# Pinning the output projection's first two passes between the steps of attention, and moving x2's first transposes

## The chip, the cores and the metric

The kernel runs on one core of one Trainium2 chip. The metric is the device time in microseconds of one execution. The time before is the median of three runs, 719.41 us (718.87 to 719.6).

## The reference

One layer of a hybrid decoder on x of 512 tokens by 1024 features, float32:

```python
h = rms_norm(x, norm_mix); proj = h @ w_in
y_a = gdn_mixer(...)      # 6 heads, gated DeltaNet: chunk solves and a scan
y_b = nsa_mixer(...)      # 6 heads, 3 per key/value head
y_c = pool_mixer(...)     # causal pooling, 4 windows
y = concatenate([y_a, y_b, y_c])          # 384 + 384 + 256 = 1024
x = x + y @ w_out
h = rms_norm(x, norm_ffn)
x = x + square(relu(h @ w_ffn1)) @ w_ffn2
```

In `nsa_mixer` each head adds three attentions: over compressed blocks, over selected blocks (with 512 tokens all blocks are chosen, so it is causal attention) and over a window of 512 (causal attention again, with other keys and values), each times a gate. What matters here is that each of the six heads needs two softmaxes over 512 x 512 causal scores and their products with the values, and that `y @ w_out` sums over eight blocks of 128 features: blocks 0 to 2 from DeltaNet, 3 to 5 from attention (two heads each), 6 and 7 from pooling.

## The kernel before, in words

**Stages.** Input projection, DeltaNet solves and scan, compression and pooling run until about 241 us. Then `gdn_out` (line 922) turns the four row blocks of the DeltaNet output, and line 1272 runs two tracks beside each other: `attentions()` and `out_gdn()`, the first part of the output projection. Lines 1311 to 1320 finish the projection, norm the sum x2 (`x2_norm`, line 1277) and transpose it (`x2_T`, line 1296); line 1334 on is the FFN, which takes the rest of the span.

**Who sets the order.** The Python code traces instructions; `side_by_side` (line 945) interleaves the tracks by the costs that they yield and their weights, a yield of -1 meaning "blocked until another track has traced what I need" (`until`, line 996). Then a scheduler of the framework gives each engine its order: it runs the traced program on a clock of its own and takes, for each engine, the earliest traced instruction that is ready. On the chip each engine then works through its own list in that order. `kp` (line 150) pins an instruction behind the one traced just before it on its engine, so that the scheduler can't move it ahead. Instructions that aren't pinned can still be taken earlier.

**Attention.** A step is one head and one of two branches (h, br), twelve steps in all. `probs` (line 1102) makes, for each of four row blocks, scores in one of two PSUM banks (0 and 1): two matmuls and a mask matmul (lines 1110 to 1112), a maximum on VectorE (1114), an exponential on ScalarE (1116); then the sums are turned into scales (1119, 1120), and two blocks are scaled on VectorE (1125) and two on ScalarE (1123). `values` (line 1127) works through three groups of blocks (`BLKS`): transposes on TensorE into bank 2 or 6 (1139), a copy to high parts on ScalarE and the rest on VectorE (`split_rows`, 147 and 148; the third group a plain copy, 1142), then the products (1155) into the head's bank. `in_turn` mixes one step's `values` with the next step's `probs`. A head's bank alternates between 7 and 3 (`pa`, line 1064); it is begun by the compressed branch's product (1179) and read by `finish` (1184).

**The DeltaNet output.** `gdn_out` transposes each row block into bank 3 (`go`, line 70; line 936) and splits it in three pieces, each a copy on ScalarE and a subtraction on VectorE (line 938 through 147 and 148).

**The output projection.** `PASS` (line 1220) has three passes over feature blocks: (6, 7), (0, 1, 2), (3, 4, 5). `out_mm` (line 1227) issues three matmuls for each feature block (1233): high by high, high by low, low by high. `out_tile` does one row block and one half of the columns and adds it to x2 on VectorE (1238); a pass has eight such tiles. Passes one and two run in `out_gdn`, unpinned: 48 and 72 matmuls. The third is begun inside the very last step (5, 1): `out_begin` pins the first two feature blocks of four tiles there, one tile behind each group's transposes; the rest is pinned from line 1312 on, with `x2_T(0)` behind the fifth tile and `x2_T(1)` behind the seventh. Weights come by `load_w` (line 1204): a DMA on SP's queue into one of two raw buffers, then a ScalarE copy and a VectorE subtraction. Blocks 4 to 7 share four tiles, blocks 0 to 3 six. Behind the projection's weights `out_gdn` loads the first two of the FFN (line 1270). PSUM banks of the pieces are `po` (line 1225): 4 and 5 for pass one, 4, 5 and 6 for pass two, 4, 5, 0, 1 for pass three.

Of the kernel before, what the change touches and what calls it, by code (L numbers as in the profile page):

```python
# [20 lines left out]
P = 128  # L21
T = 512
D = 1024
NT = T // P
# [13 lines left out]
def trunk_kernel(ctx, tc, x, norm_mix, w_in, conv_w, a_log, dt_bias, gdn_norm, nsa_q_norm, nsa_k_norm,  # L38
# [18 lines left out]
    def banks(*ids):  # L57

        c = [0]

        def get():
            b_ = ids[c[0] % len(ids)]
            c[0] += 1
            return bank.tile([P, 512], F32, tag=f"b{b_}", name=nm("ps"))

        return get
# [282 lines left out]
    ps = pn()  # L349
# [595 lines left out]
    def side_by_side(*tracks):  # L945


        tracks = [[0.0, n, g] for n, g in tracks]
        while tracks:
            blocked = set()  # L950
            while True:
                if len(blocked) == len(tracks):
                    blocked.clear()
                t = min((t for t in tracks if id(t) not in blocked), key=lambda t: t[0] / t[1])
                c = next(t[2], None)
                if c is None:
                    tracks.remove(t)
                    break
                if c >= 0:
                    t[0] += c  # L960
                    break
                blocked.add(id(t))
# [33 lines left out]
    def until(*names):  # L996
        while not have.issuperset(names):
            yield -1
# [128 lines left out]
    def values(acc, h, br, Ps):  # L1127

        end = (h, br) == (H - 1, 1)
        keep = kp if end else lambda m: m
        if end:
            yield from until("w_out")
        for b, blks in enumerate(BLKS):
            n = len(blks) * P
            tp = pt_()
            for c, (k, i) in enumerate(blks):
                keep(PE.transpose(tp[:, ts(c, P)], Ps[i][:, ts(k, P)], ident))  # L1139
            if b == 2:  # L1140
                pt = [nw.tile([P, n], F32, tag=f"pt{b}", name=nm("pt"))]
                S.copy(pt[0], tp[:, :n])
            else:
                pt = [nw.tile([P, n], F32R, tag=f"pt{c}{b}", name=nm("pt")) for c in "hl"]
                split_rows(pt[0], pt[1], tp[:, :n])
            yield 0.4
            if end:
                out_begin()
            c = 0
            while c < len(blks):  # L1150
                k, i = blks[c]
                m = sum(1 for x_ in blks if x_[0] == k)
                for p_ in pt:
                    v_ = Vt[k][:, 2 * br + h // 3]
                    keep(PE.matmul(acc[0:64 if b == 2 else P, i * P:(i + m) * P],  # L1155
                                   v_ if b == 2 else v_.rearrange("p c d -> p (c d)"),
                                   p_[:, c * P:(c + m) * P], start=False, stop=(br == 1 and b == 2),
                                   skip_group_check=True))
                c += m
            yield 0.4  # L1160
        if end:
            out_begin()

    def attentions():
        G.memset(f32v(VCz), 0.0)
        for h in range(H):
            r = slice(32 * (h % 3), 32 * (h % 3) + 32)
            S.copy(VCz[r, h], f32v(VC[r, h // 3]).rearrange("p c d -> p (c d)"))
        last = iter(())
        for h in range(H):  # L1170
            if h % 3 == 0:
                pcT[h // 3] = cmp_probs(h // 3)
            acc = pa()
            for br in range(2):
                Ps = []
                yield from in_turn((probs(h, br, Ps), last))
                if br == 0:
                    for n_, p_ in enumerate(pcT[h // 3]):
                        PE.matmul(acc, VCz[:, h], p_, start=n_ == 0, stop=False, skip_group_check=True)
                last = values(acc, h, br, Ps)  # L1180
            last = finish(last, h, acc)
        yield from last
# [32 lines left out]
    def load_wo(*cs):  # L1215
        for c in cs:
            wo[c] = load_w(wop[c < 4], w_out[0, ts(c, P), :].unsqueeze(1), "wo", "AV")

    w1s = []
    PASS = [(6,7),(0,1,2),(3,4,5)]  # L1220

    def load_w1(q):
        return load_w(wq, w_ffn1[0, :, 256 * q:256 * q + 256].rearrange("(k p) n -> p k n", p=P), "w1", "AV")

    po = banks(4, 5), banks(4, 5, 6), banks(4, 5, 0, 1)

    def out_mm(ps, cl, n0, n1, i, hf, keep=lambda m: m):

# [7 lines left out]
    def out_add(ps, i, hf):  # L1236
        cs = slice(512 * hf, 512 * hf + 512)
        V.tensor_tensor(x2[i][:, cs], ps, x2[i][:, cs], ALU.add)

    def out_tile(cl, i, hf):  # L1240
        ps = po[cl[-1] < 6]()
        out_mm(ps, cl, 0, len(cl), i, hf)
        out_add(ps, i, hf)

# [2 lines left out]
    def out_begin():  # L1247

        g_ = len(begun)
        begun.append(po[2]())  # L1250
        out_mm(begun[g_], PASS[-1], 0, 2, g_ // 2, g_ % 2, kp)

    def out_part(cl, hf):

        for i in range(NT):
            out_tile(cl, i, hf)
            yield 0.64 * len(cl)

    def out_gdn():
        for cl in PASS[:-1]:  # L1260
            load_wo(*cl)
            if cl is PASS[0]:
                for i in range(NT):
                    SY.dma_start(x2[i], x[0, ts(i, P), :])
            yield from until(*(("y", c) for c in cl if 2 < c < 6))
            for hf in range(2):
                yield from out_part(cl, hf)
        load_wo(*PASS[-1])
        have.add("w_out")
        w1s.extend(load_w1(q) for q in range(2))  # L1270

    side_by_side((42, attentions()), (27, out_gdn()))
    pt_, pm = banks(2, 6), banks(3, 7, 5)
    h2h = [t2([P, T], "h2h", F32R) for _ in range(KC)]
    h2l = [t2([P, T], "h2l", F32R) for _ in range(KC)]

# [19 lines left out]
    def x2_T(i, dg):  # L1296

        for hf in range(2):
            tp = pt_()
            for k in range(4):  # L1300
                if i < NT - 1:
                    kp(PE.transpose(tp[:, ts(k, P)], dg[hf][:, ts(k, P)], ident))
                else:
                    kp(PE.matmul(tp[:, ts(k, P)], x2[i][:, ts(4 * hf + k, P)], dg, start=True, stop=True))
            ks = [(k, vT[:, 70 + k:71 + k], tp[:, ts(k % 4, P)]) for k in range(4 * hf, 4 * hf + 4)]
            for k, gk, t_ in ks:
                S.activation(h2h[k][:, ts(i, P)], t_, AF.Copy, scale=gk)
            for k, gk, t_ in ks:
                V.scalar_tensor_tensor(h2l[k][:, ts(i, P)], t_, gk, f32v(h2h[k][:, ts(i, P)]), ALU.mult, ALU.subtract)

    dg = {}
    for g_ in range(2 * NT):
        i, hf = divmod(g_, 2)
        ps = begun[g_] if g_ < len(begun) else po[2]()
        out_mm(ps, PASS[-1], 2 if g_ < len(begun) else 0, 3, i, hf, kp)
        out_add(ps, i, hf)
        if hf:
            dg[i] = x2_norm(i)
        if g_ in (4, 6):
            x2_T(g_ // 2 - 2, dg[g_ // 2 - 2])  # L1320


    NE = 8
# [145 lines left out]
```

## Time and profile before

| | us |
|---|---|
| median of 3 runs | 719.41 |
| lowest and highest run | 718.87, 719.6 |
| the profiled execution | 720.17 |
| its span, first to last instruction | 718.2 |

The profile is of one execution. Its times are from the span's start. PE is TensorE, PEld its weight loads, DVE VectorE, ACT ScalarE, POOL GpSimd. A busy TensorE need not be at its peak: a matmul's recorded duration overlaps that of the next, so the time from start to start tells what one costs. Idle time and what ended it stand in brackets in the timeline.

### The profile page before, as it was taken

What the parts mean: (1) busy time and instruction counts of PE and PEld (TensorE: products, weight loads), DVE (VectorE), ACT (ScalarE), POOL (GpSimd) and SP (SyncE); (2) the same over time, 40 slices, a digit from 0 to 9 for tenths busy, and PEclk for the clock granted to TensorE, in tenths of its full rate; (3) what the DMA queues carried; (4) which work ended last, traced back from release to release, by engine and by line L of the source; (5) the groups of instructions that cost most, each with busy time, mean ns of one, the idle gap of its engine ahead of it and who ended that gap; (6) DMA issues with size and microseconds to landing.
All of it is one profiled execution on the core that took longest, in us unless ns stands there. A gap on an engine that the chain in (4) does not pass through costs nothing.

```text
span 718.2 us, 13258 instructions
## 1 busy us (share of the span) xinstructions
PE 693.4 (97%) x5137; PEld 568.4 (79%) x5137; DVE 552.7 (77%) x1038; ACT 389.7 (54%) x774; POOL 170.9 (24%) x257
## 2 busy tenths in 40 slices
PE   8999999999979898999889999999999999999997
PEld 8888777888979776776669888888888888888885
DVE  6689998888786669877456996968868586886836
ACT  5466845564744558676555754445444534634430
POOL 6820023312112400000020240605041140504123
PEclk9999999999999999999999999999999999999999
DMA  6343213132301502220102423333131423312103
GB/s 223 97 132 89 74 45 90 31 113 68 109 3 32 230 6 90 88 89 1 59 4 85 154 82 126 109 117 117 49 129 58 146 89 118 117 58 68 52 1 117
DMA packets 49922, 62.20 MB, mean 87 GB/s; under 512 B 5494, under 2 KB 42564, under 8 KB 49860
## 3 DMA queue, kind: packets, MB, share of 16 engines
q1 hardware_dynamic: 48996, 61.16, 26.6%
q8 instruction: 40, 0.66, 0.4%
q10 hardware_dynamic: 864, 0.20, 0.1%
q14 instruction: 22, 0.18, 0.1%
HBM read 59.25 MB, written 2.10 MB: 85 GB/s over the span
## 4 chain that ended last, share of the span: by engine, by line
PE 83%; DVE 8%; ACT 4%; DMA 3%; issue 1%; POOL 1%; SPq 0%; DVEq 0%; ACTq 0%; POOLq 0%
PE ps L1330 24%; PE ps L142 10%; PE ps L143 10%; PE ps L144 10%; PE ps L434 7%; PE ps L1233 4%; PE ps L809 3%; PE ps L1155 2%; PE ps L260 2%; PE ps L1139 1%; PE ps L597 1%; DMA raw<-in_cmp_w_dram 1%; DMA raw<-in_w_in_dram 1%; ACT P L1116 1%; PE ps L1110 1%
## 5 line engine op out<-in xcount | busy, mean ns | idle before, releaser
L1330 PE MATMUL ps<-h2h,lw 128*128 128x512 f32 (+1 forms) x280 | 104.7, 374 | 0.0
L1330 PE MATMUL ps<-h2l,hw 128*128 128x512 f32 (+1 forms) x280 | 104.7, 374 | 0.0
L1330 PE MATMUL ps<-h2h,hw 128*128 128x512 f32 (+1 forms) x280 | 104.5, 374 | 0.0
L142 PE MATMUL ps<-bh,ah 128*128 128x512 f32 x224 | 88.2, 394 | 0.5 <-DVE x L1438 0.5
L143 PE MATMUL ps<-bl,ah 128*128 128x512 f32 x224 | 88.1, 393 | 0.0
L1357 POOL TENSOR_TENSOR al<-gF,ah 128x512 fp32r<-128x512 f32 x24 | 34.3, 1430 | 223.7 <-ACT ah L1356 180.8
L1438 DVE TENSOR_TENSOR x<-ps,x 128x512 f32<-128x512 f32 x112 | 73.1, 682 | 18.6 <-PE ps L144 18.5
L144 PE MATMUL ps<-bh,al 128*128 128x512 f32 x224 | 84.8, 393 | 0.0
L1350 DVE TENSOR_TENSOR bl<-w2r,bh 128x1024 fp32r<-128x1024 f32 x40 | 57.4, 1436 | 5.6 <-ACT bh L1349 5.6
L1330 PEld LDWEIGHTS ps<-h2l,hw 128*128 128x128 f32 x280 | 52.6, 188 | 10.1
L1330 PEld LDWEIGHTS ps<-h2h,hw 128*128 128x128 f32 x280 | 52.6, 188 | 10.1
L1330 PEld LDWEIGHTS ps<-h2h,lw 128*128 128x128 f32 x280 | 52.6, 188 | 9.9
L1357 POOL TENSOR_TENSOR al<-gS,ah 128x512 fp32r<-128x512 f32 x32 | 56.7, 1790 | 15.8 <-ACT ah L1356 14.5
L1349 ACT CAST bh<-w2r 128x1024 fp32r<-128x1024 f32 x40 | 41.7, 1048 | 33.3 <-PE ps L144 33.1
L134 DVE TENSOR_TENSOR lo<-raw,hi 128x512 fp32r<-128x512 f32 (+1 forms) x76 | 43.0, 587 | 10.9 <-ACT hi L133 10.4
L133 ACT CAST hi<-raw 128x512 fp32r<-128x512 f32 (+1 forms) x76 | 37.3, 518 | 25.6 <-DMA raw<-in_w_in_dram 9.3
L142 PEld LDWEIGHTS ps<-bh,ah 128*128 128x128 f32 x224 | 42.1, 188 | 10.5 <-ACT ah L1356 0.9
L143 PEld LDWEIGHTS ps<-bl,ah 128*128 128x128 f32 x224 | 42.1, 188 | 9.7
L144 PEld LDWEIGHTS ps<-bh,al 128*128 128x128 f32 x224 | 42.1, 188 | 9.7
L133 ACT CAST hw<-raw 128x1024 fp32r<-128x1024 f32 x32 | 32.2, 1046 | 25.7 <-PE ps L1330 23.6
L134 DVE TENSOR_TENSOR lw<-raw,hw 128x1024 fp32r<-128x1024 f32 x32 | 39.1, 1255 | 6.9 <-ACT hw L133 6.8
L1356 ACT CAST ah<-gS 128x512 fp32r<-128x512 f32 x32 | 19.9, 622 | 39.7 <-DVE gS L1420 19.9
(373 smaller groups left out, 1677.8 us busy)
## 6 DMA issues: line engine op xcount, KB each, us to landing
raw<-in_w_ffn_dram SPq DMA_DIRECT2D x32, 512.0 KB, 3.8
w2r<-in_w_ffn_dram SPq DMA_DIRECT2D x32, 512.0 KB, 4.4
raw<-in_w_in_dram SPq DMA_DIRECT2D x24, 256.0 KB, 3.0
raw<-in_w_in_dram SPq DMA_DIRECT2D x36, 128.0 KB, 2.5
x<-in_x_dram SPq DMA_DIRECT2D x8, 512.0 KB, 5.9
raw<-in_cmp_w_dram SPq DMA_DIRECT2D x32, 128.0 KB, 2.8
raw<-in_w_out_dram SPq DMA_DIRECT2D x8, 512.0 KB, 4.3
out_dram<-x SPq DMA_DIRECT2D x8, 256.0 KB, 2.0
```

Of the source, the lines that this page charges most:

```text
L133: {"A": S.copy, "V": V.tensor_copy, "G": G.tensor_copy}[e[0]](hi[:, k], r)
L134: {"V": V, "G": G}[e[1]].tensor_tensor(lo[:, k], r, f32v(hi[:, k]), ALU.subtract)
L142: PE.matmul(ps, ah, bh, start=start, stop=False, **kw)
L143: PE.matmul(ps, ah, bl, start=False, stop=False, **kw)
L144: PE.matmul(ps, al, bh, start=False, stop=stop, **kw)
L434: PE.matmul(ps[:, ts(i, 256)], a_[:, k, ts(2 * b + i, P)], w_, start=(k == 0 and n_ == 0 and i == 0), stop=(k == KC - 1 and n_ == 2 and i ...
L1233: keep(PE.matmul(ps, a_[c][:, ts(i, P)], wo[c][w_][:, 0, cs], start=n_ == 0 and m_ == 0, stop=n_ == len(cl) - 1 and m_ == 2))
L1330: keep(PE.matmul(ps[:, tok], w[w_][:, k, ts(f, P)], a_[k][:, tok], start=k == 0 and m_ == 0, stop=k == KC - 1 and m_ == 2))
L1349: S.copy(hi, src)
L1350: V.tensor_tensor(lo, src, f32v(hi), ALU.subtract)
L1357: G.tensor_tensor(lo, src, f32v(hi), ALU.subtract)
L1438: V.tensor_tensor(x2[i][:, cs], acc[bk, t_], x2[i][:, cs], ALU.add)
```

## The change

- `values` is cut in two: `turned` (transposes and the split) and `product`. For head 0 the order stays: transposes, products, three times, unpinned.
- From head 1 on, everything that `values` issues on TensorE is pinned, and the order is: transposes of group 0, of group 1, some pieces of the projection, products 0, transposes of group 2, a piece, products 1, a piece, products 2. "Some" is two, but one at (2, 0).
- A piece is one feature block of one tile, three matmuls, pinned. `out_fill` hands out 32 of them: 8 for the second half of pass one, 24 for pass two; when a tile's last piece is issued its addition follows. In the last step (5, 1) the pieces are `out_begin`'s as before.
- `out_gdn` itself keeps only the first half of pass one unpinned, and the loads: blocks 6 and 7; then 0, 1, 2; then 4 and 5 when pass one has been traced; then 3 when block 0 has been used for the last time, and the FFN's first weights behind that.
- Pass three sums blocks 4, 3, 5 in that order. All pieces of passes one and two use banks 4 and 5. The track's weight goes from 27 to 24.
- `x2_T(0)` stands behind the sixth tile of pass three instead of the fifth; x2's transposes use banks 2, 6, 4 instead of 2 and 6.

```diff
-        keep = kp if end else lambda m: m
-        if end:
-            yield from until("w_out")
-        for b, blks in enumerate(BLKS):
+        keep = kp if h else lambda m: m
+
+        def turned(b):
+            blks = BLKS[b]
...
+        if h == 0:
+            for b in range(3):
+                pt = turned(b)
+                yield 0.4
+                product(b, pt)
+                yield 0.4
+            return
+        yield from until("w_out" if end else "w_012" if h > 1 else "half")
+
+        def beside(n):
+            if end:
+                out_begin()
+            else:
+                for _ in range(n):
+                    next(fill, None)
+
+        m = 1 if (h, br) == (2, 0) else 2
+        pts = [turned(0)]
+        yield 0.4
+        pts.append(turned(1))
+        yield 0.4
+        beside(m)
+        product(0, pts[0])
+        yield 0.4
+        pts.append(turned(2))
+        yield 0.4
+        beside(1)
+        product(1, pts[1])
+        yield 0.4
+        beside(1)
+        product(2, pts[2])
+        yield 0.4
         if end:
             out_begin()
...
-    PASS = [(6,7),(0,1,2),(3,4,5)]
+    PASS = [(6, 7), (0, 1, 2), (4, 3, 5)]
...
-    po = banks(4, 5), banks(4, 5, 6), banks(4, 5, 0, 1)
+    po = banks(4, 5), None, banks(4, 5, 0, 1)
...
+    def out_fill():
 
         for i in range(NT):
-            out_tile(cl, i, hf)
-            yield 0.64 * len(cl)
+            ps = po[0]()
+            for n_ in range(2):
+                out_mm(ps, PASS[0], n_, n_ + 1, i, 1, kp)
+                if n_:
+                    out_add(ps, i, 1)
+                    if i == NT - 1:
+                        have.add("first")
+                yield
+        for g_ in range(2 * NT):
+            ps = po[0]()
+            for n_ in range(3):
+                out_mm(ps, PASS[1], n_, n_ + 1, g_ // 2, g_ % 2, kp)
+                if n_ == 0 and g_ == 2 * NT - 1:
+                    have.add("filled")
+                if n_ == 2:
+                    out_add(ps, g_ // 2, g_ % 2)
+                yield
...
     def out_gdn():
...
+        load_wo(*PASS[0])
+        for i in range(NT):
+            SY.dma_start(x2[i], x[0, ts(i, P), :])
+        for i in range(NT):
+            out_tile(PASS[0], i, 0)
+            yield 1.28
+        have.add("half")
+        load_wo(*PASS[1])
+        have.add("w_012")
+        yield from until("first")
+        load_wo(4, 5)
+        yield from until("filled")
+        load_wo(3)
         have.add("w_out")
         w1s.extend(load_w1(q) for q in range(2))
 
-    side_by_side((42, attentions()), (27, out_gdn()))
-    pt_, pm = banks(2, 6), banks(3, 7, 5)
+    side_by_side((42, attentions()), (24, out_gdn()))
+    pt_, pm = banks(2, 6, 4), banks(3, 7, 5)
...
-        if g_ in (4, 6):
-            x2_T(g_ // 2 - 2, dg[g_ // 2 - 2])
+        if g_ in (5, 6):
+            x2_T(g_ - 5, dg[g_ - 5])
```

## Rows read from the trace of the kernel before

**Rows 1.** The page's head and its first part: the span, and each engine's busy time, its share of the span and its instructions (here TensorE).

```profile
span 718.2 us, 13258 instructions
...
PE 693.4 (97%) x5137; PEld 568.4 (79%) x5137; DVE 552.7 (77%) x1038; ACT 389.7 (54%) x774; POOL 170.9 (24%) x257
```

**Rows 2.** The windows by stage: the stretch in us from the span's start, its length, then busy us and instructions of TensorE (PE), its weight loads (PEld), VectorE (DVE), ScalarE (ACT) and GpSimd (POOL), the granted clock, the DMA share and GB/s.

```profile
241.00:300.00 59.00, 53.91 (x389) 39.99 (x389) 50.47 (x142) 42.33 (x111) 4.40 (x6) 1.00 0.32 115
300.00:358.00 58.00, 54.41 (x284) 38.53 (x285) 39.29 (x85) 38.77 (x95) 0.00 (x0) 1.00 0.17 55
```

**Rows 3.** The windows again, same columns, of three stretches inside the attention stage (the third overlaps the second).

```profile
258.00:270.00 12.00, 12.00 (x99) 9.20 (x99) 6.26 (x14) 6.22 (x17) 0.00 (x0) 1.00 0.00 0
270.00:300.00 30.00, 26.86 (x155) 19.36 (x153) 28.42 (x81) 24.23 (x64) 1.02 (x1) 1.00 0.28 89
277.30:357.20 79.90, 73.18 (x394) 52.08 (x392) 60.31 (x144) 56.48 (x141) 1.02 (x1) 1.00 0.21 67
```

**Rows 4.** The windows of line 1233 alone, the output projection's matmuls: busy us and number of matmuls (PE) and of weight loads (PEld) in each stretch.

```profile
241.00:258.00 17.00, 6.97 (x24) 4.17 (x24) 1.00 0.62 243
258.00:270.30 12.30, 5.90 (x23) 3.85 (x22) 1.00 0.00 0
270.30:277.30 7.00, 3.15 (x9) 1.31 (x8) 1.00 0.26 77
```

**Rows 5.** The timeline of TensorE in the last step of attention (head 5, second branch), 350 to 357.7 us.

```profile
350.03 0.66 PE L1139 MATMUL ps<-ident,P 128*128 128x128 f32 x4
350.44 0.48 PE L1233 MATMUL ps<-hwo,yTh 128*128 128x512 f32 x1
...
351.90 0.69 PE L1155 MATMUL ps<-pt,Vt 128*128 128x512 f32 x2
...
354.26 0.78 PE L1155 MATMUL ps<-pt,Vt 128*128 128x384 f32 x4
...
355.04 0.48 PE L1233 MATMUL ps<-hwo,yTh 128*128 128x512 f32 x1
...
356.61 0.65 PE L1155 MATMUL ps<-pt,Vt 128*64 128x256 f32 x2
357.18 0.50 PE L1233 MATMUL ps<-hwo,yTh 128*128 128x512 f32 x1
```

**Rows 6.** The timeline of TensorE, two score blocks: the widest (512 columns) from its first matmul to the next block's, and the narrowest (128 columns) to the matmul that follows it.

```profile
275.94 0.39 PE L1110 MATMUL ps<-XT,XT 128*128 128x512 f32 x1
...
276.44 0.31 PE L1110 MATMUL ps<-XT,XT 128*128 128x128 f32 x1
...
276.74 0.48 PE L1233 MATMUL ps<-lwo,yTh 128*128 128x512 f32 x1
```

**Rows 7.** The timeline of TensorE, 271 to 304 us: start, duration in us, engine, line, operation, output<-input, tile and number of instructions merged in the row, and in brackets the idle time before it with what ended it. The first and the last of the four groups of DeltaNet output transposes (line 936), then head 1's first matmuls into its bank.

```profile
271.95 0.49 PE L936 MATMUL ps<-ident,vb 128*128 128x128 f32 x3
...
295.68 0.52 PE L936 MATMUL ps<-ident,vb 128*128 128x128 f32 x3 [0.18 <-DVE yTl L148]
...
302.06 0.63 PE L1179 MATMUL ps<-pcT,VCz 96*128 96x512 f32 x2
302.52 1.14 PE L1155 MATMUL ps<-pt,Vt 128*128 128x512 f32 x6
```

**Rows 8.** The timeline of VectorE: the maximum of the same widest score block.

```profile
345.63 0.69 DVE L1114 TENSOR_REDUCE mx<-ps 128x1 f32<-128x512 f32 x1 [0.43 <-PE ps L1112]
```

**Rows 9.** The timeline of ScalarE behind the last scores of attention: the exponential of the widest block with its accumulator read, and the two scalings.

```profile
346.88 0.69 ACT L1116 ACTIVATE P<-ps,mx 128x512 f32<-128x512 f32 x1
347.46 0.19 ACT L1116 ACTIVATION_READ_ACCUMULATOR P<-ps,mx 128x1 f32 x1
...
348.28 1.25 ACT L1123 ACTIVATE P<-P,sm 128x384 f32<-128x384 f32 x2
```

**Rows 10.** The timeline of VectorE, same columns: three of the twelve subtractions that make the low halves of the DeltaNet output, two neighbours and the last.

```profile
292.67 0.29 DVE L148 TENSOR_TENSOR yTl<-ps,yTh 128x128 fp32r<-128x128 f32 x1 [0.54 <-ACT yTh L147]
...
293.65 0.28 DVE L148 TENSOR_TENSOR yTl<-ps,yTh 128x128 fp32r<-128x128 f32 x1
...
300.74 0.28 DVE L148 TENSOR_TENSOR yTl<-ps,yTh 128x128 fp32r<-128x128 f32 x1
```

**Rows 11.** The timeline of VectorE: the last of the four splits of the first FFN weights.

```profile
316.03 1.23 DVE L134 TENSOR_TENSOR lw<-raw,hw 128x1024 fp32r<-128x1024 f32 x1 [0.59 <-ACT hw L133]
```

**Rows 12.** The timeline of TensorE in the output projection's third pass and the first FFN matmuls, 364 to 386 us: x2's transposes are lines 1302 and 1304.

```profile
367.06 1.73 PE L1302 MATMUL ps<-ident,xn 128*128 128x128 f32 x8 [2.32 <-ACT xn L1290]
368.43 0.78 PE L1233 MATMUL ps<-hwo,yTh 128*128 128x512 f32 x1
...
370.71 0.43 PE L1233 MATMUL ps<-hwo,yTl 128*128 128x512 f32 x1
...
373.75 1.04 PE L1302 MATMUL ps<-ident,xn 128*128 128x128 f32 x8
374.54 0.48 PE L1233 MATMUL ps<-hwo,yTh 128*128 128x512 f32 x1
...
384.33 2.05 PE L1304 MATMUL ps<-dg,x 128*128 128x128 f32 x16 [0.90 <-DVE dg L1293]
```

**Rows 13.** The timeline of ScalarE: the two halves of the first row block of the normed x2.

```profile
366.28 1.33 ACT L1290 ACTIVATE xn<-x,rx 128x512 f32<-128x512 f32 x2 [1.68 <-POOL rx L1286]
```

**Rows 14.** The windows, same columns as above, of one us in the third pass; the granted clock is the number behind the five engines.

```profile
369.00:370.00 1.00, 1.00 (x4) 0.80 (x3) 0.00 (x0) 1.00 (x4) 0.00 (x0) 0.50 0.00 0
```

More of the change, by code (lines that the diff above doesn't have):

```diff
@@ L1145, in values, with product @@
                 split_rows(pt[0], pt[1], tp[:, :n])
-            yield 0.4
-            if end:
-                out_begin()
+            return pt
+        def product(b, pt):
+            blks = BLKS[b]
             c = 0
@@ L1159, in values @@
                 c += m
-            yield 0.4
+        if h == 0:
[28 more added lines that the diff above has]
+        yield 0.4
         if end:
@@ L1240, in out_tile @@
     def out_tile(cl, i, hf):
-        ps = po[cl[-1] < 6]()
+        ps = po[0]()
         out_mm(ps, cl, 0, len(cl), i, hf)
@@ L1251, in out_begin @@
         out_mm(begun[g_], PASS[-1], 0, 2, g_ // 2, g_ % 2, kp)
-    def out_part(cl, hf):
+    def out_fill():
         for i in range(NT):
-            out_tile(cl, i, hf)
-            yield 0.64 * len(cl)
-    def out_gdn():
[L1260 to L1268, printed above, removed]
+            ps = po[0]()
[7 more added lines that the diff above has]
+        for g_ in range(2 * NT):
+            ps = po[0]()
+            for n_ in range(3):
[5 more added lines that the diff above has]
+                yield
+    fill = out_fill()
+    def out_gdn():
+        load_wo(*PASS[0])
[11 more added lines that the diff above has]
+        load_wo(3)
         have.add("w_out")
         w1s.extend(load_w1(q) for q in range(2))
-    side_by_side((42, attentions()), (27, out_gdn()))
-    pt_, pm = banks(2, 6), banks(3, 7, 5)
+    side_by_side((42, attentions()), (24, out_gdn()))
+    pt_, pm = banks(2, 6, 4), banks(3, 7, 5)
     h2h = [t2([P, T], "h2h", F32R) for _ in range(KC)]
```

## The prediction

> **What bounds the kernel now.** I read the page's first part, then the windows by stage, then the timelines of TensorE, VectorE and ScalarE. TensorE is busy nearly throughout [rows 1], but "busy" overlaps from matmul to matmul, so the stages tell more. The change touches 241 to 387 us alone: attention beside the first two output passes (241 to 358), then the third pass, the norm of x2 and the first FFN matmuls. In 241 to 358 TensorE has 53.91 + 54.41 of 117 us, VectorE 50.47 + 39.29, ScalarE 42.33 + 38.77 [rows 2]. No engine is full: 8.7 us of TensorE's time are idle, so this stage is set by chains between three engines in turn. Within it the limit moves: from 258 to 270 TensorE is full (12.00 of 12) while VectorE has 6.26; from 270 to 300 VectorE is full (28.42 of 30) [rows 3]. That is where an order can gain or lose.
>
> **Part 1: fill leaves the end of head 0.** Output-projection matmuls now run wherever the scheduler found room: 24 by 258 us, 22 or 23 more by 270.3, 8 or 9 more by 277.3, when head 1's transposes begin [rows 4]. After the change only the 24 of pass one's first half stay free; the other 120 of the 144 before 358.9 are tied behind head 1's first transposes. Six matmuls take 1.46 us (350.44 to 351.90), 0.243 each [rows 5]. So 22 x 0.243 = 5.3 us leave a stretch where TensorE was the full engine: -5.3. The other 8 lie where VectorE is full [rows 3], worth nothing. Bounds -7.3 and 0; I take -5.3.
>
> **Part 2: the fill comes back between the steps of heads 1 to 5.** From 277.3 to 357.2 the kernel spends 79.9 us with 73.18 busy [rows 3], 6.7 idle. About 30 matmuls more come in: +7.3. What can pay for them is that idle time. The last step of head 5 already has the new form, pieces pinned between transposes and products, and from 350.03 to 357.18 it shows no idle mark [rows 5]: 7.15 us, of which 18 matmuls are 4.37 and the rest, ten transposes and the products, 2.78. A middle step has 12 matmuls (2.92) and beside them the next step's scores: 0.50 for the widest block, 0.30 for the narrowest [rows 6], with 0.37 and 0.43 for the two between as my estimate 1.60. Sum 7.3. Eight such, one piece less in head 2, head 5's first step with one piece (5.1), its second (7.15), ten compressed products of 0.23 (two from 302.06 to 302.52) [rows 7] and some 2 for head 3's compressed scores (an estimate by their number) give 74.2: -5.7 if nothing waits.
>
> Something will wait: a step's first transposes need the scaled probabilities. After the last score come a maximum of 0.69 [rows 8], an exponential of 0.69 with its 0.19 read, two short VectorE operations and two ScalarE scalings of 1.25 [rows 9], about 3.4 with hand-overs. Between that score and those transposes stand the second products with two transposes (354.26 to 355.04, 0.78), the third product (356.61 to 357.18, 0.57) [rows 5], two pieces of 0.73 and a score of 0.30: 3.1. So 0.3 to 1.0 us a step stay open, and over 2 in head 5's first step, which has almost no fill. Bounds: -5.7 (no wait) to +7.3 (no idle time recovered). I take the recorded idle time as what is recovered: +7.3 - 6.7 = +0.6, which is about those 74.2 with 0.5 a step and 2 in head 5.
>
> **Part 3: a wait that the pins add.** Head 1 sums in PSUM bank 3, the bank that gated DeltaNet's output transposes (L936) use. They run at 271.95 to 295.68; the last low half is subtracted at 300.74 [rows 10], and head 1's first product into its bank is at 302.06, followed by products that had been piling up [rows 7]. Now that costs little, because the free fill matmuls run meanwhile. Pinned, they stand behind head 1's first product, and TensorE does not pass it. The product would be due at 277.3 - 5.3 + 3.0 (eight transposes, two scores, six matmuls) = 275.0. The four row blocks of the DeltaNet output can start at 271.95 - 5.3 = 266.7, since the scan's last matmuls queue behind the same fill. Each block is a group of transposes (0.25) and three pairs of a ScalarE copy and a VectorE subtraction in turn; two neighbouring subtractions start 0.98 apart [rows 10], so 3.2 a block, bank free at 279.5, wait 4.5. Bounds: pairs at their bare duration, about 0.57 (a subtraction is 0.28 to 0.29, and I put the copy at the same), give 2.0 a block and no wait; today's stretch of 29.1 gives 20.8. I take 4.5, since VectorE loses two of its five weight splits and most additions of 270 to 300, and while TensorE waits little else queues in front.
>
> Of what else moves: weight chunks 0 to 2 are asked for behind pass one's first half, a head before their use; 4, 5 and 3 and the first FFN weights go later on SP's queue and ScalarE's and VectorE's. FFN splits, now at 297 to 317 (1.23 on VectorE each [rows 11]), fall beside head 5, where VectorE has room [rows 2]; one may land in the norm's chain. +0.4, bounds 0 and 2.5. Banks 4 and 5 for all pieces alternate and are cleared by one addition per six or nine matmuls: 0.
>
> **Part 4: x2's first transposes behind the sixth pair.** TensorE now stops 2.32 us for the normed x2 at 367.06 [rows 12], with ScalarE writing it from 366.28 [rows 13]. Nine matmuls of the sixth pair (2.2) fit in that gap: -2.0. The clock is 0.50 just after the stop, the 1.2 GHz level [rows 14]: five matmuls from 368.43 to 370.71 take 2.28 instead of 1.2, the eight transposes 1.37 against 0.79 at 373.75 [rows 12]. Without the gap: -1.1 and -0.3 (part of the transposes' time waits for the second half). The sixth pair being done earlier, the third block's norm starts earlier, ScalarE is clear when the fourth block comes, and the 0.90 stop at 384.33 [rows 12] goes: -0.9. Late is then ScalarE, with squares, norms and copies of two blocks in a row; TensorE's next matmuls want the copies about when they are ready. -4.3 here, bounds -4.5 and -1.5.
>
> The Trainium skill (TensorE: Matmul & The Clock Gate, section "What's actually happening") says that the array's clock falls to half when the engine has been idle and comes back with work. The trace agrees (0.50 after the 2.32 us stop). By that rule the new wait of part 3 would be paid for twice, since TensorE would restart slowly; at the 1.4 us that the tail shows, the sum would be 716.7 instead of 715.3.
>
> **Sum.** -5.3 + 0.6 + 4.5 + 0.4 - 4.3 = -4.1. The profiled execution took 720.17 us, span 718.2 and 1.97 around it: 716.07. It lies 0.76 above the median of the runs, 719.41, so the runs' median should be **715.3**.
>
> **Rivals.** *Bank 3 stays taken* (slower): the DeltaNet blocks drag as now. Midway between 3.2 and today's 7.3 a block, 5.2, bank 3 is free at 287.5, the wait 12.5, 8.0 over the forecast: 723.3, and about 724.7 with a slow restart. It turns the sum from a wait of 8.6 on, bank 3 free at 283.6. For it: today's spacing, and that VectorE is full just there. Against: much of that load is fill and splits that move away. *The pins recover nothing* (slower): steps wait for their probabilities as today, part 2 is +7.3: 722.0. This is also the case that the change doesn't do what it says, since ScalarE's and VectorE's queues are still the scheduler's. *Everything is covered*: part 2 at -3.5 and a wait of 1: 707.7; for it, the unbroken last step of head 5. *The tail is lost* (no change): FFN splits and the crowded ScalarE eat part 4, about 719.3.
>
> **How the numbers follow.** Forecast 0.42 (712 to 718 by itself), everything covered 0.15, bank 3 0.23, nothing recovered 0.08, tail lost 0.12. Range 708.0 to 726.0: it reaches over bank 3's price and nearly to full cover, and leaves out a drag as long as today's and all terms at their best. A measurement of this kernel can tell about 0.2%, 1.4 us. Faster 0.56 (forecast nearly whole, full cover), within 0.2% 0.14, slower 0.30.
>
> **What would show it.** Part 1: head 1's first transposes near 272 instead of 277.3. Part 2: no idle mark over 1 us from head 2 to head 4, steps of 7.5 to 8. Part 3: TensorE's idle time before head 1's first product, ended by the last DeltaNet subtraction; over 8.6 us there proves the forecast wrong. Part 4: no 2 us stop before x2's first transposes, clock 1.00 after them, fourth block's transposes without a stop. The prediction is also wrong if FFN splits stand between the squares and the normed x2.

## The result: slower by 1.0%

| | before | after |
|---|---|---|
| median of 4 runs, us | 719.14 | 726.34 |
| lowest and highest | 718.35, 719.6 | 725.33, 726.93 |
| profiled execution, span | 720.17, 718.2 | 725.33, 723.4 |

The kernel before was run once more here than for the median above. The ratio is 1.0099, with a 95% interval of 1.0087 to 1.0111. In the kernel after, the output projection's matmuls are line 1266, the products 1156, the compressed product 1212, x2's transposes 1356 and 1358; the transposes of P stay 1139 and DeltaNet's 936.

The span grew by 5.2 us, and three points divide it. Head 1's first transposes start at 273.78, where before it was 277.30 [rows 3, 4]: -3.5. From there to the end of attention's last product it is 273.78 to 365.45, 91.7 us, where it was 79.9 (277.30 to 357.18 [rows 3, 5]): +11.8. What follows is shorter by 3.1 (718.2 - 357.18 = 361.0 before, 723.4 - 365.45 = 358.0 after). The windows of after show where the middle part lost it (columns as in [rows 2]):

```profile
260.00:270.00 10.00, 8.79 (x69) 6.57 (x67) 7.53 (x24) 8.52 (x23) 0.00 (x0) 1.00 0.00 0
270.00:280.00 10.00, 8.22 (x44) 5.88 (x43) 10.00 (x31) 8.68 (x24) 1.00 (x1) 1.00 0.49 158
280.00:290.00 10.00, 5.54 (x20) 3.79 (x20) 3.79 (x11) 2.93 (x10) 0.00 (x0) 0.69 0.01 2
290.00:300.00 10.00, 10.00 (x59) 7.62 (x57) 7.16 (x14) 8.16 (x18) 0.00 (x0) 0.97 0.11 17
300.00:310.00 10.00, 7.01 (x39) 5.15 (x39) 9.05 (x24) 5.83 (x14) 0.00 (x0) 1.00 0.44 141
310.00:320.00 10.00, 8.59 (x49) 6.26 (x49) 8.85 (x20) 7.99 (x19) 0.00 (x0) 1.00 0.22 63
```

From 270 to 280 VectorE is full. From 280 to 290 no engine is full: TensorE 5.54 of 10 at a granted clock of 0.69, VectorE 3.79, ScalarE 2.93. That is a chain in which everybody waits. TensorE's timeline of after names it (start, duration, engine, line, output<-input, tile, and in brackets the idle time before the row with what ended it):

```profile
263.61 0.50 PE L936 MATMUL ps<-ident,vb 128*128 128x128 f32 x3
...
271.74 0.48 PE L1266 MATMUL ps<-hwo,yTh 128*128 128x512 f32 x1
...
273.44 0.50 PE L936 MATMUL ps<-ident,vb 128*128 128x128 f32 x3
273.78 1.04 PE L1139 MATMUL ps<-ident,P 128*128 128x128 f32 x8
...
279.83 0.81 PE L1139 MATMUL ps<-ident,P 128*128 128x128 f32 x4 [0.50 <-DVE P L1125]
281.58 0.52 PE L936 MATMUL ps<-ident,vb 128*128 128x128 f32 x3 [0.94 <-DVE yTl L148]
284.12 0.88 PE L936 MATMUL ps<-ident,vb 128*128 128x128 f32 x3 [1.59 <-DVE yTl L148]
286.92 1.22 PE L1212 MATMUL ps<-pcT,VCz 96*128 96x512 f32 x2 [1.93 <-DVE yTl L148]
287.94 1.05 PE L1156 MATMUL ps<-pt,Vt 128*128 128x512 f32 x2
288.79 0.63 PE L1139 MATMUL ps<-ident,P 128*128 128x128 f32 x2
289.07 0.78 PE L1266 MATMUL ps<-hwo,yTh 128*128 128x512 f32 x1
289.64 0.63 PE L1266 MATMUL ps<-lwo,yTh 128*128 128x512 f32 x1
...
299.26 0.83 PE L1072 MATMUL ps<-KCT,XT 128*128 128x64 f32 x6
...
308.79 0.44 PE L1110 MATMUL ps<-XT,XT 128*128 128x384 f32 x1 [2.07 <-ACT P L1116]
...
365.45 0.50 PE L1266 MATMUL ps<-hwo,yTh 128*128 128x512 f32 x1
```

The third and the fourth block of DeltaNet's output and then head 1's first product (286.92, its compressed one) take bank 3 one behind the other, and each waits for the subtractions of the one before. On VectorE's timeline those are the second block's three, far apart while VectorE is full, and then the last block's at its bare pace of 0.62; between them stands VectorE's half of the split that head 1's own product needs (277.34):

```profile
276.21 0.28 DVE L148 TENSOR_TENSOR yTl<-ps,yTh 128x128 fp32r<-128x128 f32 x1
...
277.34 0.68 DVE L148 TENSOR_TENSOR pt<-ps,pt 128x512 fp32r<-128x512 f32 x1
...
278.47 0.28 DVE L148 TENSOR_TENSOR yTl<-ps,yTh 128x128 fp32r<-128x128 f32 x1
...
281.16 0.28 DVE L148 TENSOR_TENSOR yTl<-ps,yTh 128x128 fp32r<-128x128 f32 x1
...
285.95 0.29 DVE L148 TENSOR_TENSOR yTl<-ps,yTh 128x128 fp32r<-128x128 f32 x1 [0.33 <-ACT yTh L147]
286.57 0.29 DVE L148 TENSOR_TENSOR yTl<-ps,yTh 128x128 fp32r<-128x128 f32 x1 [0.33 <-ACT yTh L147]
```

For the first block it is ScalarE as much as VectorE: from 266 to 272 both are all but full, ScalarE 6.00 of 6 us and VectorE 5.87.

```profile
266.00:272.00 6.00, 4.78 (x25) 3.13 (x25) 5.87 (x17) 6.00 (x18) 0.00 (x0) 1.00 0.17 48
```

Bank 3 is free at 286.86. Behind the product come, in the fixed order, head 1's third transposes (288.79) and a piece. The piece's matmuls start 0.57 and 0.43 apart, at the lower clock (0.50 in each us from 284 to 290), where 0.243 is the pace at the higher one [rows 5]. Between 273.78 and the end of attention the idle marks sum to 12.3 us: 5.0 of them from 279.83 to 286.92, 4.4 more from 301.32 to 317.66.

The tail did what it was to do (TensorE, after): no stop of 2.32 us before x2's transposes as in [rows 12], no slow clock behind them (1.00 from 375 to 378).

```profile
375.29 1.27 PE L1356 MATMUL ps<-ident,xn 128*128 128x128 f32 x8 [0.23 <-ACT xn L1344]
...
384.03 0.39 PE L1384 MATMUL ps<-h2l,hw 128*128 128x256 f32 x1 [0.42 <-DVE h2l L1363]
```

### The profile page after: what moved, and what is told of

The parts are those of the page before. It is cut to its first block, busy times and chain, and to the rows that moved or that the text cites. A ratio compares the mean times of both kernels' runs of the same rounds, so it can differ in the third digit from the quotient of the medians.

```text
span 723.4 us, 13252 instructions
## 1 busy us (share of the span) xinstructions
PE 694.0 (96%) x5137; PEld 569.6 (79%) x5137; DVE 553.9 (77%) x1038; ACT 390.9 (54%) x774; POOL 171.0 (24%) x257
## 4 chain that ended last, share of the span: by engine, by line
PE 81%; DVE 8%; ACT 4%; DMA 3%; issue 3%; POOL 1%; SPq 0%; DVEq 0%; ACTq 0%; POOLq 0%
PE ps L1384 24%; PE ps L142 10%; PE ps L143 10%; PE ps L144 10%; PE ps L434 6%; PE ps L1266 3%; PE ps L809 2%; PE ps L1156 2%; DMA raw<-in_w_ffn_dram 2%; PE ps L260 2%; PE ps L597 1%; PE ps L1139 1%; DVE mx L1114 1%; DMA raw<-in_w_in_dram 1%; DVE lwo L134 1%
## 5 line engine op out<-in xcount | busy, mean ns | idle before, releaser
L134 DVE TENSOR_TENSOR lo<-raw,hi 128x512 fp32r<-128x512 f32 (+1 forms) x76 | 42.8, 586 | 11.3 <-ACT hi L133 9.7
L142 PEld LDWEIGHTS ps<-bh,ah 128*128 128x128 f32 x224 | 42.1, 188 | 10.5 <-ACT ah L1410 0.9
```

What stands on the lines that cost most here:

```text
L134: {"V": V, "G": G}[e[1]].tensor_tensor(lo[:, k], r, f32v(hi[:, k]), ALU.subtract)
L142: PE.matmul(ps, ah, bh, start=start, stop=False, **kw)
```

## The experiments

Times are medians; each ratio is to the kernel before on the same chip, with its 95% interval.

**1. Is the tail a gain of its own?** The kernel before with the last part alone, and the kernel after without it:

```diff
-    pt_, pm = banks(2, 6), banks(3, 7, 5)
+    pt_, pm = banks(2, 6, 4), banks(3, 7, 5)
-        if g_ in (4, 6):
-            x2_T(g_ // 2 - 2, dg[g_ // 2 - 2])
+        if g_ in (5, 6):
+            x2_T(g_ - 5, dg[g_ - 5])
```

> The kernel before with the last part of the change alone: x2's first transposes behind the fifth and sixth tile, three banks for them. Theory (the tail is a gain of its own, read as 3.6 us from the changed kernel's trace between the last product and the fourth block's FFN): 715.5, from 715.0 to 716.0. Rival (the gain comes only with the order that the fixed pieces leave behind, or is given back in the FFN): 718.5 to 719.5.

> The changed kernel with its last part undone: x2's first transposes behind the fourth and sixth tile again, and two banks. Theory (the tail is worth 3.6 to 3.9 us whatever stands ahead of it): 726.3 + 3.7 = 730, from 729 to 731, with a stop of about 2 us ahead of x2's first transposes. Rival (the gain of the tail depends on what the rest leaves): 726 to 728.

716.16, ratio 0.9946 (0.993 to 0.9963); and 730.39, ratio 1.0153 (1.0138 to 1.0168). The stop before x2's transposes is 0.22 us in the one and is back in the other (`e3`, then `e4`):

```profile
365.79 1.27 PE L1302 MATMUL ps<-ident,xn 128*128 128x128 f32 x8 [0.22 <-ACT xn L1290]
```

```profile
377.08 1.27 PE L1356 MATMUL ps<-ident,xn 128*128 128x128 f32 x8 [2.33 <-ACT xn L1344]
```

So the tail is worth 3.9 to 4.1 us on either side, and the rest of the change costs 10 to 11.

**2. Bank 3, the order, or head 1?** Three edits of the kernel after. ScalarE empties bank 3 at once (`e1`); nothing fixed before head 5's last step (`e5`); head 1 as before the change, its pieces given to heads 2 to 5 (`e6`):

```diff
# e1, in gdn_out: copy out of the bank, split from there
+        of = o.rearrange("p h d -> p (h d)")
+        S.copy(of, ps[:, 0:3 * P])
         for j in range(3):
-            split_rows(..., ps[:, ts(j, P)])
+            split_rows(..., of[:, ts(j, P)])
# e5
-        keep = kp if h else lambda m: m
+        keep = kp if end else lambda m: m
# e5: and no kp on the two out_mm calls in out_fill
# e6
+        keep = kp if h > 1 else lambda m: m
-        if h == 0:
+        if h < 2:
# e6: and five pieces a step behind it
```

> The four transposed blocks of the delta rule's output are copied out of bank 3 by one ScalarE copy into their own input tile, and split from there, so bank 3 no longer waits for VectorE's subtractions. Theory (head 1's first product waits for bank 3): in the changed kernel the product is ready at 278.0 and starts at 286.92; the fourth block's rsqrt chain still ends at 278.0, its transposes could be done near 280 and the copy near 281, so the wait falls from 10 us to 3 or 4 and the kernel ends near 719 to 721, some 6 us below the changed kernel. Rival (VectorE is the bound of this stretch, whatever the bank does): the transposes of head 1 and the products are served by VectorE as before, and the time stays at 725 to 727. Rival (the fixed order itself costs the time): same, 725 to 727.

> The changed kernel with the same pieces and passes traced at the same places, but nothing fixed in program order before head 5's last step. Theory (the wait for bank 3 costs so much because the fill is locked behind head 1's products): the fill runs in the wait, and the time falls to 715 to 719. Rival (the wait itself is on the chain whatever is traced around it, or the passes' split into pieces costs): 724 to 727.

> The changed kernel with head 1 as the kernel before had it (nothing fixed, no piece of the fill beside it); its eight pieces go to heads 2 to 5, five pieces a step. Theory (the loss is at head 1 alone): the 8 to 10 us stop at head 1's first product goes or shrinks to that of before, heads 2 to 5 keep their fixed order, and the time is 716 to 720. Rival (fixing the order costs all along heads 1 to 5): at least 723, with stops spread over heads 2 to 5.

`e1`: 723.78, ratio 1.0053 (1.003 to 1.0076), only 2.6 us below after (3.3 by the ratios). `e5`: 714.49, ratio 0.9924 (0.9906 to 0.9941). `e6`: 716.52, ratio 0.9955 (0.9935 to 0.9974). The fixed order costs, and it costs at head 1; heads 2 to 5 fixed cost little. But `e1` falls short of its theory. Its product did come 7.5 us earlier, and yet the last product ends only 2.0 us earlier (363.47 against 365.45). TensorE still stands 4.8 us between 300 and 318 (4.4 in after), and ScalarE stands there, ahead of the exponential that is wanted, for raw FFN weights (TensorE, then ScalarE, of `e1`):

```profile
279.42 1.21 PE L1214 MATMUL ps<-pcT,VCz 96*128 96x512 f32 x2 [0.77 <-ACT vb L938]
...
304.91 0.50 PE L1112 MATMUL ps<-XT,XT 128*128 128x512 f32 x1 [0.76 <-ACT P L1118]
...
308.92 0.33 PE L1112 MATMUL ps<-XT,XT 128*128 128x128 f32 x1 [2.00 <-ACT P L1118]
```

```profile
307.25 1.04 ACT L133 CAST hw<-raw 128x1024 fp32r<-128x1024 f32 x1 [2.40 <-DMA raw<-in_w_ffn_dram]
```

**3. Which part of the order?** The fill alone free (no `kp` in `out_fill`); transposes and products alone free (`keep = kp if end`); and, for `e1`'s stop, a third buffer for raw weights beside the early bank (`pool("wr", 3)`).

> The changed kernel with the pieces of the fill not fixed, the transposes and products of heads 1 to 5 still fixed. Theory (what costs is that the fill stands locked behind a product that waits): the pieces run in head 1's wait and in the stops of heads 2 and 3, and the time falls to 715 to 719. Rival (the fixed order of the transposes and products, with the scores, is what costs): 724 to 727.

> The changed kernel with the transposes and products of heads 1 to 5 not fixed, the pieces of the fill fixed where they are traced. Theory (locked fill): a piece is fixed to the instruction that is traced just before it, a transpose or a product, so the fill is still held back where that one waits; the time stays above before, 720 to 726. Rival (the fixed transposes and products cost): 715 to 718.

> Bank 3 released early as in the run of that name (ScalarE copy), and three instead of two buffers for the raw weight blocks. In the run with the bank alone the first product of head 1 came 7.5 us earlier but the end of the last step only 2 us: between 300 and 320 ScalarE stood 1.5 to 2.4 us at a time for a raw block of the FFN's weights with the scores' exponentials queued behind it. Theory (that wait ate the gain): with a third buffer the blocks are there, and the time falls to 717 to 720, from 723.8. Rival (the stops at 300 to 320 belong to head 3's compressed softmax and VectorE): 722 to 725.

`e9`: 723.55, ratio 1.0061 (1.0044 to 1.0078). `e10`: 716.05, ratio 0.9957 (0.9942 to 0.9972). My theory, that the loss is the fill locked behind the product, falls: freed, the fill brings 2.8 us; left fixed, with the rest free, the loss is gone. `e11`: 721.95, ratio 1.0028 (1.0016 to 1.0041), 1.8 below `e1`, but the two intervals overlap. The third buffer also only shortened ScalarE's three longest waits for raw FFN blocks, from 1.53, 2.40 and 1.68 us in `e1` to 0.27, 0.82 and 2.14. So the run does not say what these waits cost in full.

**4. The transposes.** A new theory: a fixed transpose stands behind the product, and with it all that needs the transpose. Only the transposes of P free in heads 1 to 5; then, as tests of the bank, the fourth block delayed by four passes of GpSimd over it, in the kernel after and in `e5`; and `e5` with the early bank.

```diff
# e15
-                keep(PE.transpose(tp[:, ts(c, P)], Ps[i][:, ts(k, P)], ident))
+                (kp if end else lambda m: m)(PE.transpose(...))
# e16, e17, in gdn_out
+        for _ in range(4 if i == 3 else 0):
+            G.tensor_copy(o, o)
```

> The changed kernel with only the transposes of P (heads 1 to 5, all but the last step) not fixed; products and pieces of the fill stay fixed. Of the earlier runs the one with the fill free gained 2.8 us, the one with transposes and products free 10.3. Theory (a fixed transpose stands behind the product that waits for bank 3, and with it the scores and exponentials of the next steps): with the transposes free they run ahead of that product, and the time is 715.5 to 717.5. Rival (it is the products' own order that costs, where they stand in front of the scores): 722 to 726.

> The changed kernel with the fourth block of the delta rule's output delayed on GpSimd alone, by four more passes over it that change nothing (GpSimd is idle there); an estimate of 4 us later in bank 3. Theory (head 1's first product waits for that block and all else stands behind it): the product starts some 4 us later than 286.92, and the time grows by 2 to 4 us, to 728 to 730. Rival (the wait is given back behind it, the stops at 300 to 320 being set by the weights and VectorE): 725.5 to 727.

> The same delay of the fourth block in the kernel with nothing fixed before head 5's last step (714.49). Theory (unfixed, transposes, scores and fill run while bank 3 is taken): no more than 0.7 us slower, 713.5 to 715.2. Rival (the wait is on the chain there too): 716 to 718.5.

> Nothing fixed before head 5's last step, and bank 3 released early by ScalarE's copy. Theory (unfixed, the wait for bank 3 costs nothing): 713.5 to 715.5, the same as without the early release. Rival (the bank still costs some of its time): 711 to 713.

`e15`: 715.26, ratio 0.9943 (0.9922 to 0.9963): the transposes carry nearly all of the loss. `e16`: 727.43 (724.42 to 729.24), ratio 1.0102 (1.0075 to 1.013), which says nothing on the price of the wait: the four passes took GpSimd only 2.35 us and the fourth block had been waiting for the bank anyway, so head 1's product came at 287.28. `e17`: 713.78, ratio 0.9914 (0.9899 to 0.9929), no loss, but the delay hardly arrived: head 1's product starts at 306.22, and in `e5`, without the delay, at 305.44. That second number is worth more than the test (TensorE of `e5`):

```profile
305.44 0.73 PE L1212 MATMUL ps<-pcT,VCz 96*128 96x512 f32 x2 [0.94 <-DVE yTl L148]
306.00 3.51 PE L1156 MATMUL ps<-pt,Vt 128*128 128x512 f32 x16
```

With nothing fixed, bank 3 comes free some 18.5 us later than in after (product at 305.44 against 286.92), sixteen products wait for it and run in one go, and the kernel is 11.9 us faster.

`e12`: 720.74, ratio 1.0015 (1.0005 to 1.0026), 6 us slower than `e5`, where I expected nothing. Its output-projection matmuls are gone by 310 (windows of that line alone: matmuls, weight loads, clock):

```profile
300.00:310.00 10.00, 5.08 (x18) 3.34 (x18) 1.00 0.34 103
310.00:320.00 10.00, 0.00 (x0) 0.00 (x0) 0.63 0.57 194
320.00:330.00 10.00, 0.00 (x0) 0.00 (x0) 0.86 0.00 1
```

and those of `e15` are not:

```profile
310.00:320.00 10.00, 3.51 (x12) 2.03 (x12) 1.00 0.31 100
320.00:330.00 10.00, 4.50 (x15) 2.54 (x15) 1.00 0.34 100
```

`e5` has spent its fill by 310 too, and is fast; so that alone does not explain `e12`.

**5. Which head's transposes?** Fixed in head 1 alone (`keep = kp if h == 1 or end`); free in head 1 alone (`keep if h > 1` on the transpose); and a candidate, `e5` with a third raw buffer.

> The changed kernel with transposes and products fixed in head 1 alone (and in head 5's last step, as before the change); those of heads 2 to 5 free, the pieces of the fill fixed where they are traced. All free gave 716.05, all fixed 726.3, and with head 1 as the kernel before had it 716.52. Theory (the loss is made at head 1, where the fixed transposes stand behind the product that waits for bank 3, and is not made up later): 723 to 727. Rival (half of it or more is lost in head 2's and head 3's steps, by their own fixed order, whatever head 1 did): 716 to 721.

> The changed kernel with the transposes of head 1 alone not fixed; its products, all of heads 2 to 5 and the fill stay fixed. Theory (the loss is made by head 1's transposes): 715 to 718, as with all transposes free (715.26). Rival (the steps of heads 2 and 3, which meet the weights' splits and head 3's compressed softmax, lose it by their own fixed order): 720 to 726.

> Nothing fixed before head 5's last step (714.49), and three buffers for the raw weight blocks. A candidate. If ScalarE's waits for raw blocks cost there too: 712 to 713.8. If they are covered: 714 to 715.5. The early release of bank 3, which was to cost nothing, made this kernel 6 us slower by using the fill up before 310, so a kernel whose fill runs out earlier still: 717 to 721.

`e19`: 727.13, ratio 1.0109 (1.0093 to 1.0125). `e20`: 715.85, ratio 0.9946 (0.9928 to 0.9965). This settles the place: the twenty transposes of head 1 make nearly the whole loss; with them free, the rest of the fixed order leaves 1.4 us to `e5` (1.6 by the ratios). `e14`: 715.61, ratio 0.9946 (0.9931 to 0.9961), no better than `e5`. Now `e20` against after; its windows:

```profile
280.00:290.00 10.00, 9.34 (x63) 7.20 (x61) 9.09 (x30) 9.01 (x28) 1.02 (x1) 1.00 0.04 17
290.00:300.00 10.00, 9.53 (x47) 6.81 (x47) 8.64 (x25) 6.67 (x18) 0.00 (x0) 1.00 0.00 0
300.00:310.00 10.00, 10.00 (x60) 8.00 (x59) 8.90 (x15) 7.12 (x17) 0.00 (x0) 1.00 0.33 107
```

and its TensorE, in rows that answer to those of after:

```profile
280.04 0.38 PE L1139 MATMUL ps<-ident,P 128*128 128x128 f32 x2
280.18 0.47 PE L1266 MATMUL ps<-hwo,yTh 128*128 128x512 f32 x1
...
286.28 1.16 PE L1139 MATMUL ps<-ident,P 128*128 128x128 f32 x8
287.30 0.86 PE L1072 MATMUL ps<-KCT,XT 128*128 128x64 f32 x6
...
291.30 0.71 PE L1212 MATMUL ps<-pcT,VCz 96*128 96x512 f32 x2
...
355.20 0.50 PE L1266 MATMUL ps<-hwo,yTh 128*128 128x512 f32 x1
```

Head 1's product starts *later* than in after, 291.30 against 286.92, and the kernel is 10.5 us faster. The wait is not shorter; it has work in it. Head 1's third transposes run at 280.04 instead of 288.79, the piece behind them at 280.18 instead of 289.07, and ahead of the product go the next steps' scores and transposes and even head 3's compressed scores, 287.30 against 299.26 in after.

**6. By which link?** The third transposes empty the tiles of the two widest blocks of P, of which there are two. ScalarE of after, then of `e20`, at the third block's exponential of the step behind:

```profile
289.24 0.58 ACT L1116 ACTIVATE P<-ps,mx 128x384 f32<-128x384 f32 x1 [2.70 <-PE ps L1139]
```

```profile
281.13 0.59 ACT L1116 ACTIVATE P<-ps,mx 128x384 f32<-128x384 f32 x1
```

So two more runs, all fixed as in after: head 1's third transposes traced ahead of its first product; and a third tile for those blocks.

```diff
# e21
+        if h == 1:
+            pts.append(turned(2))
         beside(m)
         product(0, pts[0])
# e22
-            p_ = nw.tile([P, n], F32, tag=f"P{i}", name=nm("P"))
+            p_ = nw.tile([P, n], F32, tag=f"P{i}", bufs=3 if i >= 2 else 2, ...)
```

> The changed kernel, everything fixed as in it, but in head 1 the third transposes of a step are traced ahead of its first product instead of behind it. Theory (they empty the tiles of the two widest blocks of P, which two steps later's exponentials want: in the changed kernel the exponential at 289.24 waits 2.70 us for transposes that stand behind the product that waits for bank 3, with all transposes free it comes at 281.13): 714.5 to 717.5. Rival (what counts is the products' wait and the fill locked behind it): 722 to 726.

> The changed kernel with three buffers instead of two for the tiles of the two widest blocks of P, the order fixed as in it. Theory (the exponentials wait for a tile that the fixed transposes have not read): they run ahead by one step more, and 3 to 8 of the 11 us come back, 718 to 723; not all, since the next step's transposes still stand behind the products. Rival (the tiles have no part in it): 725 to 727.5.

`e21`: 722.62, ratio 1.0034 (1.0017 to 1.005). `e22`: 728.84, ratio 1.0123 (1.0093 to 1.0152). So the tiles are not the main link. With a third one the exponentials run one step further and then stand before the same wait, and head 1's product too (ScalarE, then TensorE, of `e22`):

```profile
290.89 0.58 ACT L1116 ACTIVATE P<-ps,mx 128x384 f32<-128x384 f32 x1 [2.70 <-PE ps L1139]
```

```profile
288.57 1.22 PE L1212 MATMUL ps<-pcT,VCz 96*128 96x512 f32 x2 [1.93 <-DVE yTl L148]
```

`e21` brings 3.7 of the 11 us (4.7 by the ratios), though head 3's compressed scores come at 287.17, as early as in `e20`. It loses time from 290 to 300 (its product waits 1.15 us at 294.34, and TensorE has 7.47 of 10) and from 330 to 340 (8.45 of 10, clock 0.83 in both). Why the second, I have not found out.

## Why the prediction was wrong

**The step that failed is part 3**, "I take 4.5, since VectorE loses two of its five weight splits and most additions of 270 to 300, and while TensorE waits little else queues in front". It failed twice.

- *The size of the wait.* Forecast: four blocks of 3.2 us, bank 3 free at 279.5. Measured: the blocks take the bank from 263.61 to 286.86, the first two 8.7 and 8.0 us while ScalarE and VectorE are busy with other work, the last two 2.4 and 2.7. The bank was free 7.4 us later than forecast, close to the rival *Bank 3 stays taken* (287.5), whose 723.3 or 724.7 stands against 726.34. The product was ready at 278.0, when VectorE ended its split (277.34 + 0.68), and started at 286.92: a wait of 8.9 us, over the 8.6 at which the sum was to turn. The sign set beforehand spoke of TensorE's idle time, and that is only 5.0, since a score, some transposes and two DeltaNet blocks still ran.
- *What stands behind the wait.* "Little else queues in front" is the half that decides. I had only the fill queued there. The transposes of P are fixed too; the runs put the loss on them (`e15`, `e19`, `e20`), and the fill alone brings 2.8 us (`e9`). The size alone does not: in `e1`, with one more ScalarE copy a block, the product starts at 279.42, where the forecast had the bank free at 279.5, and the kernel still takes 723.78. In `e5` and `e20` the wait is longer than in after, and they are among the fastest. So neither my price nor the rival's has the right reason: both take the wait for its length.

By spans, after is 9.3 us over the forecast (723.4 against 718.2 - 4.1 = 714.1). The stretch from head 1's first transposes to attention's last product has 6.7 of it: 91.7 against 79.9 + 0.6 + 4.5 = 85.0. Part 1 has 1.8, what follows attention 0.8.

The other terms are best read in `e20`, where that step is taken out. *Part 1* forecast -5.3: transposes at 273.78 in after and 274.85 in `e20`, against 277.30: -3.5 and -2.5, short by 1.8 and 2.8. A reason that the rows show for 1.5 of it: six pinned matmuls of the fill ran ahead of head 1's transposes, from 271.74 to 273.20 in after. `kp` ties a piece to the one instruction traced just before it, and not to all the transposes before it. *Part 2* forecast +0.6 on 79.9: `e20` has 80.4 (274.85 to 355.20), right in size; its sign, no idle mark over 1 us from head 2 to head 4, failed in after (2.07 at 308.79) and held in `e20`. *Part 4* forecast -4.3: 3.9 to 4.1 by `e3` and `e4`, right, and the 0.90 stop [rows 12] became one of 0.42 at another place (384.03). One side remark was wrong: the FFN's weights are not fetched beside head 5 but from 299.9 on, with their splits from 303.9 on.

That `e20` takes 715.85, where the forecast was 715.3, is luck. Without its 4.5 us of wait the forecast would have been 710.8; part 1 gave 2.8 us less, and what follows attention 1.3 less (-2.6 against -4.3 + 0.4). The tail alone (`e3`) gains 3.9 us on before and `e20` 3.6, so in `e20` the new order of attention gains nothing that the runs show. In `e5` it may be 1.7 us, but its interval and that of `e3` overlap.

The Trainium skill (TensorE: Matmul & The Clock Gate, section "What's actually happening") has the clock fall when the engine has been idle. The trace agrees, a granted clock of 0.50 in each us from 284 to 290 after the first stops, and 0.43 to 0.57 a matmul behind the last. It is not the main part: of the 11.3 us that the middle part is longer in after than in `e20`, 7.9 are idle marks (12.3 against 4.4), which leaves 3.4 for the clock and all else.

The Trainium skill (Perfetto Trace Analysis, section "Matmuls") asks for rotation through several PSUM banks. DeltaNet's four blocks use one, and TensorE did stand for it (1.59 and 1.93 us). But freeing that bank early, the nearest run to it here, gave about 3 us with the fixed order and cost about 6 without it.

**Open.** How the 11 us divide between the stop at 280 to 290 and the stretch of 300 to 320. By which link head 1's transposes make the loss: their third group accounts for 3.7 us (`e21`), the rest is not shown. Why the early bank hurts `e5`, and why `e21` loses time at 330 to 340. Each of these edits lets the scheduler lay out all that follows anew, so differences of some us between such kernels need not come from the edited spot. Eight versions beat both kernels. The fastest are the change without the fixed order, `e5` at 714.49 and, with the delay that hardly arrived, `e17` at 713.78; the tail alone gives 716.16.

## What to carry to other kernels

Before an instruction is fixed behind another, ask what the other may wait for and follow *everything* that depends on the fixed one, not only the filler that the order was made for: here twenty fixed transposes cost 11 us, and fixing the fill alone about 2 (`e10` against `e5`). A wait is priced by the work that can still run in it, not by its length. And an estimate of how soon another engine frees a buffer should use its pace where its queue is full (8.0 and 8.7 us a block here), not between such stretches (2.4 and 2.7).

## What was not expected of the hardware

One late transfer held up work on two engines that did not need it: in `e1` ScalarE stood 2.40 us for a raw weight block (307.25), with the scores' exponentials behind it, and TensorE stopped 2.00 us at 308.92 for one of those. A bank did the same on TensorE: in after, head 1's third transposes and a piece ran behind the product that waited for bank 3, at 288.79 and 289.07; in `e20`, with those transposes free, the same work ran at 280.04 and 280.18, while the bank was still taken.
